# Top-2 gate dispatch on one Trainium2 core: loads with 32 KB rows, stores with 64 and 32 KB rows, and half of each group's output expanded in place over its own input

## Chip, core and metric

The kernel runs on one core of one Trainium2 chip. The metric is the device time of one execution in microseconds (us). A profile is one execution of the program taken by the hardware profiler; its span runs from the first to the last instruction on the core and is a little shorter than the device time of the same execution. KB and MB are used as the profile does: "2048.0 KB" of a DMA is 2,097,152 bytes, and 1 MB in a rate is a million bytes.

## Reference

The inputs are `x` (16 x 1024 tokens of 512 floats), router logits (8 per token) and k = 2. For each token the two largest softmax probabilities are taken and normalised to sum to 1, and the output holds the token's row twice, each copy multiplied by one of the two weights:

```python
    topk_indices = np.argsort(probs, axis=-1)[..., -k:]
    topk_probs = np.take_along_axis(probs, topk_indices, axis=-1)
    topk_probs = topk_probs / np.sum(topk_probs, axis=-1, keepdims=True)
    x_expanded = x[:, :, np.newaxis, :].repeat(k, axis=2)
    return (x_expanded * topk_probs[..., np.newaxis]).astype(np.float32)
```

So 33.55 MB of `x` and 0.52 MB of logits are read, and 67.11 MB are written, all in float32. Which expert was chosen does not enter the output; only the two weights do, and they are the sigmoids of the difference of the two largest logits.

## The kernel before

The 16,384 tokens are laid over 128 partitions with M = 128 tokens (slots) each, so that a partition's tokens are one contiguous stretch of memory: 256 KB of `x` and 512 KB of output.

**Weights (L22 to L42).** One DMA brings all logits into the core (L76). `top2_weights` finds the largest and second largest by a tree of max and min on VectorE (DVE), and two sigmoids on ScalarE (ACT) write the weight table `WA`. This is done once.

**Groups, loads and stores.** The work goes in two groups of 64 slots. In each group all eight loads are issued first: a load (L84) brings 8 slots, 128 rows of 16 KB, 2 MB, into its own buffer `xg` (a pool of eight). Then each buffer is expanded in two halves: one DVE multiplication (L90) reads 4 slots of `xg`, broadcast over k, times their weights, and writes 4 x 2 x 512 floats per partition into a buffer `og` (a pool of four, 16 KB a partition each); a store (L98) sends `og`, 128 rows of 16 KB, to the output. So a group is eight loads of 2 MB and then sixteen stores of 2 MB.

**What sets the order.** All DMAs, loads and stores alike, are issued by SyncE (SP) in program order, and run on one queue that is spread over the core's 16 DMA engines; each engine takes 8 of the 128 rows of each DMA. The order on SP is: logits, eight loads, sixteen stores, eight loads, sixteen stores. SP stops at the first instruction whose wait is not met, and everything behind it on SP stops with it. A store waits for its multiplication. A multiplication waits for its load, and for the store that last read its `og` buffer (four stores back). A load of the second group waits until the multiplications have read its buffer. No order is written out otherwise; the tile framework adds the waits. The pools take 8 x 16 + 4 x 16 = 192 KB a partition beside the weights.

Of the kernel before, what the change touches and what calls it, by code (L numbers as in the profile page):

```python
# [1 line left out]

# [4 lines left out]

F32 = mybir.dt.float32
ALU = mybir.AluOpType
ACTF = mybir.ActivationFunctionType  # L10
P = 128


def top2_weights(nc, pool, logits, M, E):

    hi, lo, n = None, None, E
    while n > 1:  # L20
        n //= 2
        if hi is None:  # L22
            a, b = logits[:, :, 0:n], logits[:, :, n : 2 * n]
            nhi = pool.tile([P, M, n], F32, tag=f"hi{n}")
            nlo = pool.tile([P, M, n], F32, tag=f"lo{n}")
            nc.vector.tensor_tensor(nhi, a, b, op=ALU.max)  # L26
            nc.vector.tensor_tensor(nlo, a, b, op=ALU.min)  # L27
        else:
            a, b = hi[:, :, 0:n], hi[:, :, n : 2 * n]
            nhi = pool.tile([P, M, n], F32, tag=f"hi{n}")  # L30
            nlo = pool.tile([P, M, n], F32, tag=f"lo{n}")
            tmp = pool.tile([P, M, n], F32, tag=f"tmp{n}")
            nc.vector.tensor_tensor(tmp, lo[:, :, 0:n], lo[:, :, n : 2 * n], op=ALU.max)  # L33
            nc.vector.tensor_tensor(nlo, a, b, op=ALU.min)  # L34
            nc.vector.tensor_tensor(nlo, nlo, tmp, op=ALU.max)  # L35
            nc.vector.tensor_tensor(nhi, a, b, op=ALU.max)  # L36
        hi, lo = nhi, nlo
    dlt = pool.tile([P, M], F32, tag="dlt")
    nc.vector.tensor_tensor(dlt, hi[:, :, 0], lo[:, :, 0], op=ALU.subtract)  # L39
    WA = pool.tile([P, M, 2], F32, tag="WA")  # L40
    nc.scalar.activation(WA[:, :, 0], dlt, ACTF.Sigmoid, scale=-1.0)  # L41
    nc.scalar.activation(WA[:, :, 1], dlt, ACTF.Sigmoid, scale=1.0)  # L42
    return WA


@with_exitstack
def kernel(
    ctx: ExitStack,
    tc: tile.TileContext,
    x: bass.AP,  # L50
    router_logits: bass.AP,
    k: bass.AP,
    out: bass.AP,
):
    nc = tc.nc
    B, S, D = x.shape
    E = router_logits.shape[-1]
    N = B * S
    assert int(k) == 2 and E == 8 and N % P == 0
    M = N // P  # L60

    L = 8
    H = 4
    GROUP = 8
    x_v = x.rearrange("b s d -> (b s) d").rearrange("(p m) d -> p m d", p=P)
    o_v = out.rearrange("b s k d -> (b s) k d").rearrange("(p m) k d -> p m k d", p=P)
    rl_v = router_logits.rearrange("b s e -> (b s) e").rearrange(
        "(p m) e -> p m e", p=P
    )

    wpool = ctx.enter_context(tc.tile_pool(name="wpool", bufs=1))
    xbufs = ctx.enter_context(tc.tile_pool(name="xbufs", bufs=GROUP))
    obufs = ctx.enter_context(tc.tile_pool(name="obufs", bufs=4))

    logits = wpool.tile([P, M, E], F32)
    nc.sync.dma_start(logits, rl_v)  # L76
    WA = top2_weights(nc, wpool, logits, M, E)

    for g in range(M // L // GROUP):
        chunks = range(g * GROUP, (g + 1) * GROUP)  # L80
        xgs = []
        for c in chunks:
            xg = xbufs.tile([P, L, D], F32, tag="xg")
            nc.sync.dma_start(xg, x_v[:, c * L : (c + 1) * L, :])  # L84
            xgs.append(xg)
        for c, xg in zip(chunks, xgs):
            for h in range(L // H):
                rows = slice(c * L + h * H, c * L + (h + 1) * H)
                og = obufs.tile([P, H, 2, D], F32, tag="og")
                nc.vector.tensor_tensor(  # L90
                    og,
                    xg[:, h * H : (h + 1) * H, :]
                    .unsqueeze(2)
                    .to_broadcast([P, H, 2, D]),
                    WA[:, rows, :].unsqueeze(3).to_broadcast([P, H, 2, D]),
                    op=ALU.mult,
                )
                nc.sync.dma_start(o_v[:, rows], og)  # L98


# [1 line left out]
_INS = ['x', 'router_logits', 'k']  # L102
_OUTS = [((16, 1024, 2, 512), 'float32')]

_NUMBERS = {'k': 2}


# [26 lines left out]
```

## Time and profile before

| | |
|---|---|
| median of 3 runs | 243.29 us (243.09 to 243.54) |
| the profiled execution's own time | 243.44 us |
| its span | 241.7 us |
| outside the span | 1.74 us |
| DMAs | 1 for the logits, 16 loads, 32 stores, all issued by SP |
| DVE busy | 144.8 us (60% of the span), of which L90 141.1 us in 32 instructions |
| bytes over the span | 101.2 MB, 419 GB/s on the mean |

How to read it. An engine's busy share is a mean over the whole span. The profile also cuts the span into 40 slices of 6.04 us and gives for each the busy share of the DMA engines and the GB/s that they moved; packets are counted by their start, so a slice can be a packet or two off. A DMA packet here is one row of one DMA on one engine: 6144 of the packets are the 16 KB rows of loads and stores, 128 are the 4 KB rows of the logits, and 16 small ones of 4 bytes end each DMA, one on each engine, and signal that the engine's share has landed. "To landing" is the time from a DMA's issue on SP until the last of these sixteen.

The trace also gives each DMA's landings by themselves. The loads of the first group land at 9.39, 14.29, 19.18, 24.08, 28.97, 33.86, 38.77 and 45.14 us, the stores behind them at 50.02, 54.88, 59.75, 64.60 us and so on up to 118.08 and 123.37; the second group's loads at 128.15, 133.05 and so on up to 157.52 and 163.01, and its stores from 167.88 to 240.81.

### The profile page before, as it was taken

To read this page: it belongs to the slowest core of one execution; us is meant where nothing else is said; L and a number is where in the kernel's file an instruction comes from. 1 tells how busy PE (TensorE), PEld (TensorE's weight loads), DVE (VectorE), ACT (ScalarE), POOL (GpSimd) and SP (SyncE) were. 2 spreads that over 40 slices of the span, in tenths; PEclk is the share of its full clock that TensorE was granted. 3 is DMA by queue.
4 is the path that set the end of the run, shared out by engine and by line. 5 is a ranking of instruction groups with operands and counts; after the bars stand their busy time and mean duration, and the time that the engine had idled before them with its cause. 6 is when DMAs were issued, how large, how long until landed. Compare 5 with 4: busy or idle time off the path is not lost.

```text
span 241.7 us, 202 instructions
## 1 busy us (share of the span) xinstructions
DVE 144.8 (60%) x43; ACT 1.8 (1%) x3; POOL 0.2 (0%) x4
## 2 busy tenths in 40 slices
DVE  2899400078999899980007991001998989989300
ACT  2000000000000000000000000000000000000000
POOL 0000000000000000000000000000000000000000
DMA  7999999999999999999999999999999999999995
GB/s 274 420 431 434 434 434 369 404 428 434 428 434 434 428 426 431 431 434 431 434 401 428 431 434 426 423 420 431 434 434 434 431 431 427 431 434 433 431 428 233
DMA packets 7058, 101.21 MB, mean 419 GB/s; under 512 B 784, under 2 KB 784, under 8 KB 912
## 3 DMA queue, kind: packets, MB, share of 16 engines
q1 hardware_dynamic: 7056, 101.19, 98.9%
q14 instruction: 2, 0.02, 0.0%
HBM read 34.08 MB, written 67.11 MB: 419 GB/s over the span
## 4 chain that ended last, share of the span: by engine, by line
DMA 74%; DVE 17%; issue 2%; SPq 1%; DVEq 0%
DMA out_dram<-og 61%; DVE og L90 17%; DMA xg<-in_x_dram 13%; SPq L84 0%; SPq L76 0%; SPq L98 0%; DVEq L90 0%
## 5 line engine op out<-in xcount | busy, mean ns | idle before, releaser
L90 DVE TENSOR_TENSOR og<-xg,WA 128x4096 f32<-128x4096 f32 x32 | 141.1, 4423 | 76.5 <-issue 45.5
L26 DVE TENSOR_TENSOR nhi<-logits 128x512 f32<-128x512 f32 x1 | 0.7, 691 | 4.6 <-DMA logits<-in_router_logits_dram 4.6
L41 ACT ACT_TABLE_LOAD x1 | 1.3, 1283 | 0.7 <-PEq L115 0.7
L36 DVE TENSOR_TENSOR nhi<-nhi 128x256 f32<-128x256 f32 (+1 forms) x2 | 0.7, 350 | 0.0
L34 DVE TENSOR_TENSOR nlo<-nhi 128x256 f32<-128x256 f32 (+1 forms) x2 | 0.7, 350 | 0.0
L33 DVE TENSOR_TENSOR tmp<-nlo 128x256 f32<-128x256 f32 (+1 forms) x2 | 0.7, 350 | 0.0
L35 DVE TENSOR_TENSOR nlo<-nlo,tmp 128x256 f32<-128x256 f32 (+1 forms) x2 | 0.7, 350 | 0.0
L27 DVE TENSOR_TENSOR nlo<-logits 128x512 f32<-128x512 f32 x1 | 0.7, 684 | 0.0
L41 ACT ACTIVATE WA<-dlt 128x128 f32<-128x128 f32 x1 | 0.3, 315 | 6.4 <-DVE dlt L39 6.4
L39 DVE TENSOR_TENSOR dlt<-nhi,nlo 128x128 f32<-128x128 f32 x1 | 0.3, 292 | 0.0
L42 ACT ACTIVATE WA<-dlt 128x128 f32<-128x128 f32 x1 | 0.3, 298 | 0.0
L115 POOL MEMSET const-uint8-127<- 128x1 uint8 x1 | 0.1, 103 | 0.0
L115 POOL MEMSET const-bfloat16-1.0<- 128x1 bf16 x1 | 0.1, 102 | 0.0
L115 POOL MEMSET const-float32-0.0<- 128x1 f32 x1 | 0.1, 99 | 0.2 <-issue 0.2
L115 POOL MEMSET const-float32-1.0<- 128x1 f32 x1 | 0.1, 99 | 0.0
## 6 DMA issues: line engine op xcount, KB each, us to landing
out_dram<-og SPq DMA_DIRECT2D x32, 2048.0 KB, 14.9
xg<-in_x_dram SPq DMA_DIRECT2D x16, 2048.0 KB, 28.8
logits<-in_router_logits_dram SPq DMA_DIRECT2D x1, 512.0 KB, 3.8
```

What stands on the lines that cost most here:

```text
L26: nc.vector.tensor_tensor(nhi, a, b, op=ALU.max)
L27: nc.vector.tensor_tensor(nlo, a, b, op=ALU.min)
L33: nc.vector.tensor_tensor(tmp, lo[:, :, 0:n], lo[:, :, n : 2 * n], op=ALU.max)
L34: nc.vector.tensor_tensor(nlo, a, b, op=ALU.min)
L35: nc.vector.tensor_tensor(nlo, nlo, tmp, op=ALU.max)
L36: nc.vector.tensor_tensor(nhi, a, b, op=ALU.max)
L39: nc.vector.tensor_tensor(dlt, hi[:, :, 0], lo[:, :, 0], op=ALU.subtract)
L41: nc.scalar.activation(WA[:, :, 0], dlt, ACTF.Sigmoid, scale=-1.0)
L42: nc.scalar.activation(WA[:, :, 1], dlt, ACTF.Sigmoid, scale=1.0)
L90: nc.vector.tensor_tensor(og, xg[:, h * H : (h + 1) * H, :] .unsqueeze(2) .to_broadcast([P, H, 2, D]), WA[:, rows, :].unsqueeze(3).to_broa ...
L115: nc = _bacc.Bacc("TRN2", target_bir_lowering=False, num_devices=1)
```

## The change

The buffers of the two pools become two tiles: `xs` of 64 slots (128 KB a partition) and `osp` of 16 slot pairs (64 KB a partition). A group is still 64 slots, with all loads ahead of all stores, on the same queue. Its loads are four DMAs of 16 slots, 128 rows of 32 KB, 4 MB each. Its expansion is six multiplications and six stores, by the list `plan`:

- slots 0 to 15 go to the whole of `osp`, one store with rows of 64 KB (8 MB);
- slots 16 to 31 go to `low`, which is `xs` slots 0 to 31 seen as 16 pairs: they are expanded over the slots 0 to 15 that the first step has read and over themselves; one store with rows of 64 KB;
- slots 32 to 39 go to the first half of `osp`, 40 to 47 to its second half; two stores with rows of 32 KB (4 MB);
- slots 48 to 55 go to `xs` slots 32 to 47, and 56 to 63 to `xs` slots 48 to 63, over what has been read and over themselves; two stores with rows of 32 KB.

`low` and `high` are views of `xs`, so a load of the second group waits for the store that reads its slots. The number of bytes, the elements multiplied and the weights are the same.

```diff
-    L = 8
-    H = 4
-    GROUP = 8
+    GROUP = 64
+    L = 16
...
-    xbufs = ctx.enter_context(tc.tile_pool(name="xbufs", bufs=GROUP))
-    obufs = ctx.enter_context(tc.tile_pool(name="obufs", bufs=4))
-
...
-    for g in range(M // L // GROUP):
-        chunks = range(g * GROUP, (g + 1) * GROUP)
-        xgs = []
-        for c in chunks:
-            xg = xbufs.tile([P, L, D], F32, tag="xg")
-            nc.sync.dma_start(xg, x_v[:, c * L : (c + 1) * L, :])
-            xgs.append(xg)
-        for c, xg in zip(chunks, xgs):
-            for h in range(L // H):
-                rows = slice(c * L + h * H, c * L + (h + 1) * H)
-                og = obufs.tile([P, H, 2, D], F32, tag="og")
-                nc.vector.tensor_tensor(
-                    og,
-                    xg[:, h * H : (h + 1) * H, :]
-                    .unsqueeze(2)
-                    .to_broadcast([P, H, 2, D]),
-                    WA[:, rows, :].unsqueeze(3).to_broadcast([P, H, 2, D]),
-                    op=ALU.mult,
-                )
-                nc.sync.dma_start(o_v[:, rows], og)
+    xs = wpool.tile([P, GROUP, D], F32)
+    osp = wpool.tile([P, L, 2, D], F32)
+
+
+    low = xs[:, : 2 * L, :].rearrange("p (r k) d -> p r k d", k=2)
+    high = xs[:, 2 * L :, :].rearrange("p (r k) d -> p r k d", k=2)
+    h = L // 2
+    plan = [
+        (0, L, osp),
+        (L, L, low),
+        (2 * L, h, osp[:, :h]),
+        (2 * L + h, h, osp[:, h:]),
+        (3 * L, h, high[:, :h]),
+        (3 * L + h, h, high[:, h:]),
+    ]
+
+    for g in range(M // GROUP):
+        m0 = g * GROUP
+        for r in range(0, GROUP, L):
+            nc.sync.dma_start(xs[:, r : r + L, :], x_v[:, m0 + r : m0 + r + L, :])
+        for r, n, og in plan:
+            rows = slice(m0 + r, m0 + r + n)
+            nc.vector.tensor_tensor(
+                og,
+                xs[:, r : r + n, :].unsqueeze(2).to_broadcast([P, n, 2, D]),
+                WA[:, rows, :].unsqueeze(3).to_broadcast([P, n, 2, D]),
+                op=ALU.mult,
+            )
+            nc.sync.dma_start(o_v[:, rows], og)
```

## The prediction

> **What bounds the kernel now.** I read the page's slices first, then rates by stage, then the multiplications in order of time. The slices:
>
> ```profile
> DVE  2899400078999899980007991001998989989300
> ...
> DMA  7999999999999999999999999999999999999995
> GB/s 274 420 431 434 434 434 369 404 428 434 428 434 434 428 426 431 431 434 431 434 401 428 431 434 426 423 420 431 434 434 434 431 431 427 431 434 433 431 428 233
> ```
>
> The DMA engines are never idle from the second slice to the last but one, and move about 431 GB/s; DVE has holes. The low slices are the start (0), the end (39), and the places where the queue goes from loads to stores (6 and 7) and from stores to loads (20). The same by stage (columns: stretch, length, busy us of DVE, ACT, POOL, TensorE clock, DMA share, GB/s):
>
> ```profile
> 12.00:38.00 26.00, 14.92 (x4) 0.00 (x0) 0.00 (x0) 1.00 1.01 433
> 38.00:46.00 8.00, 0.00 (x0) 0.00 (x0) 0.00 (x0) 1.00 0.99 358
> 46.00:118.00 72.00, 53.10 (x12) 0.00 (x0) 0.00 (x0) 1.00 1.01 431
> 118.00:128.00 10.00, 0.00 (x0) 0.00 (x0) 0.00 (x0) 1.00 1.01 413
> 128.00:156.00 28.00, 17.43 (x4) 0.00 (x0) 0.00 (x0) 1.00 1.01 431
> 156.00:168.00 12.00, 0.04 (x1) 0.00 (x0) 0.00 (x0) 1.00 1.00 422
> 168.00:236.00 68.00, 53.06 (x12) 0.00 (x0) 0.00 (x0) 1.00 1.01 431
> ```
>
> Against 431, the changes of direction lose 8 x (1 - 358/431) = 1.35 us, 10 x (1 - 413/431) = 0.42 and 12 x (1 - 422/431) = 0.25: about 2.0 in all. In between, the order of time shows DVE waiting for stores, not stores for DVE:
>
> ```profile
> 54.97 4.42 DVE L90 TENSOR_TENSOR og<-xg,WA 128x4096 f32<-128x4096 f32 x1 [0.44 <-DMA out_dram<-og]
> 59.83 4.42 DVE L90 TENSOR_TENSOR og<-xg,WA 128x4096 f32<-128x4096 f32 x1 [0.43 <-DMA out_dram<-og]
> 64.69 4.43 DVE L90 TENSOR_TENSOR og<-xg,WA 128x4096 f32<-128x4096 f32 x1 [0.44 <-DMA out_dram<-og]
> ```
>
> The starts are 4.86 us apart, the time of one 2 MB store. So the bytes through the DMA engines are the bound: 101.2 MB at 431 GB/s is 234.8 us of the 241.7. The change moves the same bytes. Only the cost per packet and per DMA, the direction changes, and a gap in the queue, if it makes one, can matter.
>
> **Cost per packet.** In the trace's packet records, on one engine, the commonest distance from one 16 KB store packet to the next is 607 ns, and for the 4 KB rows of the logits 155 ns. The slope is (607 - 155)/12,288 bytes: 602.7 ns for 16 KB, which leaves 4.3 ns fixed per packet. Loads: their landings are 4.895 us apart, 611.9 ns per packet, 9.2 over the slope, and I do not know whether that excess goes with packets or with bytes. Between the last packet of one DMA and the first of the next the distance is mostly 613, so a DMA's end costs some 6 ns.
>
> Each engine has 8 rows of each DMA. Loads: 16 x 8 = 128 packets before, 8 x 8 = 64 after, 64 fewer: 64 x 4.3 = 0.28 us, or 64 x 9.2 = 0.59 if the loads' whole excess is per packet. Stores: 32 x 8 = 256 before; after, 4 with 64 KB rows and 8 with 32 KB rows, 12 x 8 = 96, 160 fewer: 160 x 4.3 = 0.69. DMAs: 49 before, 21 after, 28 x 6 ns = 0.17. Sum 1.14 to 1.45; I take 1.3. No row of this trace shows a packet above 16 KB. From below: if rows are cut at 16 KB, only the 0.17 is left. From above on this term: 1.45.
>
> The Trainium skill, "DMA: Bandwidth & Descriptors", section "Anatomy of one DMA", gives a transfer a fixed 2.0 us beside its bytes; 28 fewer would be worth 56 us, an estimate from that page, and the time 187. That section itself says that it is completion latency; in this trace stores follow each other 4.86 us apart for 8 x 602.7 ns = 4.82 us of bytes, so 0.04 us of it is on the path here. The page's section "Why small descriptors are slow" has about 3 cycles of overhead per packet, which with its 850 MHz is an estimate of 3.5 ns, and 224 fewer packets would give 0.79 us in place of the 0.97 (0.28 + 0.69) from the rows.
>
> **DVE.** Per output element (4423 - 691)/(4096 - 512) = 1.041 ns from the rows of L90 and L26, fixed 0.16 us. A step of 16 slots (16,384 outputs) is 17.2 us, of 8 slots 8.7: 4 x 17.2 + 8 x 8.7 = 138.4 in place of 141.1. All of it lies beside DMAs, so it counts nothing as long as the queue stays fed. Writing over one's own input: L35 does it (nlo<-nlo,tmp), 350 ns, as L33 and L34, which do not:
>
> ```profile
> L33 DVE TENSOR_TENSOR tmp<-nlo 128x256 f32<-128x256 f32 (+1 forms) x2 | 0.7, 350 | 0.0
> L35 DVE TENSOR_TENSOR nlo<-nlo,tmp 128x256 f32<-128x256 f32 (+1 forms) x2 | 0.7, 350 | 0.0
> ```
>
> I take no extra; L35 is small and not broadcast, so bound it by twice the step (8.7 more for 8 slots), which the margins below still cover.
>
> **Does the queue stay fed?** Larger steps mean later first stores and longer waits, so I lay the six steps (S0 to S5) out at the old rates: 64 KB stores 19.4 us, 32 KB stores 9.7, loads 9.8. Load 0 lands at 14.3 (where before the second load did). S0's multiplication ends at 31.5, S1's at 48.7. Loads end at 45.1 with the old loss of the direction change. S0's store, issued at 31.5, has 13 us in hand; it lands at 64.5, and S1's, issued at 48.7, follows to 84.0. S2 writes `osp` and must wait until S0's store has landed: this is the wait that the change adds. Behind it on DVE stand S3, S4, S5, and on SP their stores and all loads of the second group. It runs 64.6 to 73.3, and the queue needs it at 84.0: **margin 10.7 us**, the smallest of all. S3 ends at 82.0, S4 at 90.7, S5 at 99.4; their stores are needed at 93.7, 103.4, 113.1. SP then issues the second group's loads 0 and 1 at about 99.5 (their slots were freed when S1's store landed, 84.0); load 2 waits for S4's store (113.1), load 3 for S5's (122.9), with load 0 and 1 (19.6 us) queued ahead. The second group repeats it: load 0 lands near 133, S0 is multiplied by 150.3, loads end at 163; S2 runs 182.5 to 191.2 and is needed at 201.9. SP's own issues, 12 stores of 0.33 us and 8 loads of 0.47 us, are fewer than before. No margin is under 8.7, so even a doubled 8-slot step in S2 would not empty the queue. If this cover went, each microsecond past 10.7 would be lost twice, once a group.
>
> **What stays.** The start (load 0's data begins as before, behind the logits) and the tail: sixteen parts of the last store land from 238.86 to 240.81, a spread of 1.95 us that the slowest engine sets. These are the same in kind; I allow 0.5 either way.
>
> **Sum.** The profiled execution's own 243.44 (span 241.7 and 1.74 around it) less 1.3 is 242.1. The median of the runs lies 0.15 below the profiled one; from it, 243.29 - 1.3 = **242.0**, which I take.
>
> **Rivals.**
> - *The rows do not become larger packets*, or the excess goes with bytes. For: every 16 KB row is one packet, but nothing larger is seen. Against: the 4 KB and 16 KB rows differ as a fixed cost would make them. Then only 0.17 goes: 243.1.
> - *Slower: the direction changes grow with the row.* After the first group's loads each engine's first three or so store packets take 0.85 to 1.25 us in place of 0.61. If that is a loss per packet, with 64 KB rows it is four times as long where stores follow loads, 3 x (1.35 + 0.25) = 4.8 more, and with 32 KB rows twice where loads follow stores, 0.42 more: 242.0 + 5.2 = 247.2; at half of that 244.6. It decides for slower from 1.3 + 0.5 = 1.8 us extra, when the 2.0 of before becomes 3.8. Against it: the second change from loads to stores costs only 0.25 with the same rows, so it looks like engines that start in step and get out of each other's way in time, not like a price per packet.
> - *Faster than forecast: the first direction change shrinks* to the second's price, as longer rows change how engines meet: 1.1 less, 240.9. Nothing shows it but the 1.35 against 0.25.
>
> **How the numbers follow.** A difference of 0.2% (0.49 us) is about what a measurement of this kernel can tell from no change; so faster means below 242.8, slower above 243.8. Forecast (241.3 to 242.8): 0.58. No larger packets (242.8 to 243.8): 0.15. Direction changes grow: 0.17. They shrink: 0.10. Faster 0.58 + 0.10 = 0.68, same 0.15, slower 0.17. The range takes in the forecast, the no-gain case, the shrinking case down to 240.7 and the start of the slower case: 240.7 to 244.0, leaving out most of the slower case and little else.
>
> **What would show it.** Right: packet count near 2,560 beside the small ones; rates of 432 to 434 GB/s between the direction changes; no hole in the DMA row; DVE idle before S2, ended by a store. Wrong: 6,144 large packets (first rival); rates under 400 for more than 4 us around 45 and 160 us (second); a slice with DMA under 9 in the middle, which would mean that a margin above was misjudged.

## The result and the profile after

Beside the prediction's 242.0 us (240.7 to 244.0) the changed kernel took 242.67 us in the median of 4 runs (242.31 to 242.96), the kernel before 243.19 (242.86 to 243.54) next to it: ratio 0.9978, interval 0.9958 to 0.9997. With more runs even that shrank. In the next comparison (11 runs against 28) the two took 242.57 and 242.48 us, ratio 1.0001, interval 0.999 to 1.0012. The two intervals overlap only between 0.999 and 0.9997. So a gain of 0 to 0.1% is all that fits both, under what a measurement of this kernel can tell from no change; the forecast was 0.5%.

The profiled execution of the changed kernel was the fastest of its four (242.31 us, span 240.5), so the first thing to learn is not to read the gain from one pair of profiles (1.1 us here). The slices, with the page's packet count:

```profile
DVE  3279999900399999400000899998007999990000
...
DMA  8999999898989899999999999999989898999995
GB/s 327 430 409 425 430 431 425 349 523 349 523 349 523 349 436 436 436 436 431 436 338 431 436 431 430 431 474 414 458 381 490 371 501 360 431 436 436 436 436 256
DMA packets 3024, 101.19 MB, mean 421 GB/s; under 512 B 336, under 2 KB 336, under 8 KB 464
```

3024 - 464 = 2560 large packets: the rows did become packets of 32 and 64 KB. The DMA row has no hole. The pairs of 349 and 523 are not a rate: packets are counted by their start, and with 64 KB packets a slice holds two or three rounds of them. Slice 20 (338) is the change from stores to loads, and it is lower than before. By stage (stretch, length, busy us of DVE, ACT, POOL, clock, DMA share, GB/s):

```profile
12.00:38.00 26.00, 24.17 (x2) 0.00 (x0) 0.00 (x0) 1.00 1.01 435
38.00:46.00 8.00, 8.00 (x1) 0.00 (x0) 0.00 (x0) 1.00 1.02 360
46.00:118.00 72.00, 36.96 (x5) 0.00 (x0) 0.00 (x0) 1.00 1.00 433
118.00:128.00 10.00, 0.00 (x0) 0.00 (x0) 0.00 (x0) 1.00 0.99 370
128.00:156.00 28.00, 22.94 (x2) 0.00 (x0) 0.00 (x0) 1.00 1.00 432
156.00:168.00 12.00, 11.51 (x1) 0.00 (x0) 0.00 (x0) 1.00 1.02 437
168.00:236.00 68.00, 34.67 (x4) 0.00 (x0) 0.00 (x0) 1.00 1.00 432
```

Between the changes of direction the rate is 432 to 435, where the kernel before has 431 to 433 (forecast 432 to 434). The stretch with the change from stores to loads fell from 413 to 370. And the multiplications in order of time, with the group lines:

```profile
63.95 17.29 DVE L97 TENSOR_TENSOR osp<-xs,WA 128x8192 f32<-128x8192 f32 x2 [15.67 <-DMA out_dram<-osp]
...
181.60 17.29 DVE L97 TENSOR_TENSOR osp<-xs,WA 128x8192 f32<-128x8192 f32 x2 [14.10 <-DMA out_dram<-osp]
```

```profile
L97 DVE TENSOR_TENSOR osp<-xs,WA 128x8192 f32<-128x8192 f32 (+1 forms) x6 | 69.0, 11534 | 70.1 <-DMA xs<-in_x_dram 40.3
L97 DVE TENSOR_TENSOR xs<-xs,WA 128x8192 f32<-128x8192 f32 (+1 forms) x6 | 69.2, 11536 | 0.2
```

S2 waits 14 to 16 us for S0's store, starts at 63.95 (forecast 64.6) and is done at 72.6, with its store's turn at about 83. Writing in place costs nothing: 11,536 ns in xs, 11,534 in osp.

**The measure used below.** Rates in a window blur with long packets, so I use the landings in the trace. The *loss* at a change of direction is counted over two DMAs, the last of the old direction and the first of the new: how much longer they take together, by their landings, than in steady running (4.89, 9.72 and 19.35 us for loads of 2, 4 and 8 MB, 4.86, 9.68 and 19.32 for stores; where the last DMA is cut into short pieces, over all its pieces). In the changed kernel, for example, the third load lands at 33.14 us, the fourth at 44.54 and the first store at 63.85; that is 30.7 us in place of 29.0, a loss of 1.7, nearly all of it before the last load lands. Loads of 4 MB land 9.68 to 9.73 us apart, so a loss is good to some 0.03 us. There are three changes: loads to stores, stores to loads, loads to stores.

### The profile page after: what moved, and what is told of

The parts are those of the page before. It is cut to its first block, busy times and chain, and to the rows that moved or that the text cites. A ratio compares the mean times of both kernels' runs of the same rounds, so it can differ in the third digit from the quotient of the medians.

```text
span 240.5 us, 112 instructions
## 1 busy us (share of the span) xinstructions
DVE 142.0 (59%) x23; ACT 1.8 (1%) x3; POOL 0.2 (0%) x4
## 2 busy tenths in 40 slices
DMA packets 3024, 101.19 MB, mean 421 GB/s; under 512 B 336, under 2 KB 336, under 8 KB 464
## 3 DMA queue, kind: packets, MB, share of 16 engines
q1 hardware_dynamic: 3024, 101.19, 98.7%
## 4 chain that ended last, share of the span: by engine, by line
DMA 46%; DVE 36%; issue 7%; SPq 0%; DVEq 0%
DMA out_dram<-osp 27%; DVE osp L97 22%; DMA xs<-in_x_dram 19%; DVE xs L97 14%; SPq L72 0%; SPq L103 0%; DVEq L97 0%
## 5 line engine op out<-in xcount | busy, mean ns | idle before, releaser
L97 DVE TENSOR_TENSOR osp<-xs,WA 128x8192 f32<-128x8192 f32 (+1 forms) x6 | 69.0, 11534 | 70.1 <-DMA xs<-in_x_dram 40.3
L97 DVE TENSOR_TENSOR xs<-xs,WA 128x8192 f32<-128x8192 f32 (+1 forms) x6 | 69.2, 11536 | 0.2
```

What stands on the lines that cost most here:

```text
L97: nc.vector.tensor_tensor(og, xs[:, r : r + n, :].unsqueeze(2).to_broadcast([P, n, 2, D]), WA[:, rows, :].unsqueeze(3).to_broadcast([P, n, ...
```

## Why there was no gain

Taking the losses, and the time until the logits land, out of the last landing leaves the pace. Profiles of the kernel before, and of a version of the changed kernel with all rows at 16 KB (rows16 below), against those of the changed kernel (us):

| | logits land | losses in order | sum of losses | last landing | last landing less logits and losses |
|---|---|---|---|---|---|
| before | 4.56 | 1.50, 0.31, 0.58 | 2.39 | 240.81 | 233.86 |
| before_again | 4.38 | 0.69, 0.73, 0.07 | 1.49 | 239.82 | 233.95 |
| rows16 | 4.58 | 0.42, 0.54, 0.13 | 1.09 | 239.57 | 233.90 |
| after | 4.02 | 1.70, 1.34, 0.15 | 3.19 | 239.53 | 232.32 |
| after_again | 4.46 | 0.88, 1.21, 0.58 | 2.67 | 239.48 | 232.35 |

The last column is the part that the forecast worked out: 1.6 us less, 1.14 to 1.45 forecast, and it is there in each execution. The losses take it back: 1.66 on the mean of the three, 2.93 with the long rows, 1.27 more. The 0.3 us between the two are inside the scatter of the losses. Of the 1.27, the change from stores to loads has 0.75; the other 0.5 lies in the changes from loads to stores, where two executions of one kernel differ by as much (1.50 and 0.69), so these profiles do not show that the long rows caused that part. In the first pair of profiles another 0.5 us came from the logits landing early (4.02), which none of the eighteen later profiles repeats (4.22 to 4.64).

The experiments ask what sets these losses. Theory A: the rows next to the change. Theory B: chance. Theories C, D and E came up on the way. Ratios are to the kernel before on the same chip, with the 95% interval.

## Experiments: the change from stores to loads

**Both kernels again.** No edit.

> The unchanged kernel before, to see how far one execution of it differs from the next. Both theories: ratio 1.000 within 0.002. Theory A (the rows set the price of the change from stores to loads): the last store of the first group lands 5.2 to 5.4 us after the one before it, as in the first profile (5.29), a loss of 0.3 to 0.5. Theory B (the direction changes and the start scatter from one execution to the next, whatever the rows): this loss lies anywhere between 0.3 and 1.5, and the first load's landing (9.39 in the first profile) moves by up to 0.8.

> The changed kernel once more. Theory A: 0.4 to 0.7 us under the kernel before in the median; the last store of the first group lands about 11.1 us after the one before it in place of 9.69 (loss 1.2 to 1.6 again); loads and stores in between keep 9.72, 9.68 and 19.32 us; the first load lands between 13.4 and 14.3. Theory B: the same median, but the loss at that place somewhere between 0.3 and 1.5, and not tied to it.

Measured: before_again 242.41 us, 0.9995 (0.9986 to 1.0005); after_again 242.57, 1.0001 (0.999 to 1.0012). The loss from stores to loads is 0.31 and 0.73 in the two executions before, 1.34 and 1.21 in the two after. The first load's landing moved by only 0.1 in the kernel before. That speaks for A at this place; the losses from loads to stores scatter as B says (1.50 and 0.69; 1.70 and 0.88).

**The last store of each group in 16 KB rows (laststore, laststore_again).**

```diff
-            nc.sync.dma_start(o_v[:, rows], og)
+            if r == 3 * L + h:
+                for s in range(0, n, 4):
+                    nc.sync.dma_start(o_v[:, m0 + r + s : m0 + r + s + 4], og[:, s : s + 4])
+            else:
+                nc.sync.dma_start(o_v[:, rows], og)
```

> The changed kernel with the last store of each group cut into two stores with 16 KB rows. Theory A in the form that it is the stores' rows: the loss at the change from stores to loads falls from 1.5 to 0.4 to 0.8, so the time is 0.6 to 1.0 us under the changed kernel (16 more packets an engine and 2 more DMAs cost 0.08 of it). Theory A in the form that it is the loads' rows, and theory B: the time is that of the changed kernel plus 0.1, within 0.2.

> The kernel with 16 KB rows in the last store of each group, once more, beside the three below. Theory A (the price of a change of direction grows with the rows next to it): ratio to the kernel before 0.996 to 0.998 as the first time (0.9970); loss from stores to loads 0.5 to 0.9. If the first time was chance: 0.999 to 1.001.

**The first load of each group in 16 KB rows (firstload).**

```diff
-            nc.sync.dma_start(xs[:, r : r + L, :], x_v[:, m0 + r : m0 + r + L, :])
+            step = 8 if r == 0 else L
+            for s in range(r, r + L, step):
+                nc.sync.dma_start(
+                    xs[:, s : s + step, :], x_v[:, m0 + s : m0 + s + step, :]
+                )
```

> The changed kernel with the first load of each group cut into two loads with 16 KB rows. Theory A in the form that it is the loads' rows: the loss at the change from stores to loads falls from 1.5 to 0.4 to 0.8 and the time is 0.6 to 1.0 us under the changed kernel (16 more packets an engine and 2 more DMAs cost 0.1 to 0.15 of it). Theory A in the form of the stores' rows, and theory B: the time of the changed kernel plus 0.1 to 0.2.

Measured: laststore 241.77 us, 0.997 (0.9959 to 0.9982), and 241.70, 0.9977 (0.9966 to 0.9987); loss 0.70 and 0.70. firstload 242.57, 1.0007 (0.9998 to 1.0016); loss 1.26. So it is the stores' rows and not the loads'; with 4 MB of each group's 32 cut, the kernel is 0.4 to 0.7 us under the kernel before.

**Longer and shorter last stores (all64, laststore4, turns).** all64 replaces the last four steps by two with 64 KB rows; laststore4 cuts the last store into 4, 2, 1 and 1 slots; turns does that too and cuts the last load into 8, 4, 2, 1 and 1 slots, which is rows of 16, 8, 4, 2 and 2 KB (its expectation below names them twice, the second time rightly).

```diff
+        (2 * L, L, osp),
+        (3 * L, L, high),
...
+            cuts = (4, 2, 1, 1) if r == 3 * L + h else (n,)
...
+            cuts = (8, 4, 2, 1, 1) if r == 3 * L else (L,)
```

> The changed kernel with four stores a group, all with 64 KB rows: slots 32 to 47 over the whole of osp, 48 to 63 over the last half of xs. Theory A (the last stores' rows price the change from stores to loads): the loss there grows from 1.5 to 2.2 to 3.0 us; 32 fewer packets an engine and 4 fewer DMAs give 0.15 back; so 0.5 to 1.4 us over the changed kernel, about 243.0 to 244.0 where the kernel before has 242.5. Theory B (scatter): the changed kernel less 0.15. The third store's multiplication has 2.3 us in hand by the old times; if that is misjudged, the DMA row shows a hole near 84 us and it is that.

> The changed kernel with the last store of each group cut into rows of 16, 8, 4 and 4 KB (4, 2, 1 and 1 slots). Theory A: the loss at the change from stores to loads falls to 0.2 to 0.6 (0.86 with 16 KB rows, 1.5 with 32 KB); 0.1 to 0.6 under the kernel with 16 KB last stores, so a ratio to the kernel before of 0.9945 to 0.9968. Theory B or a fixed price per change: ratio 0.997 as with 16 KB last stores, or 0.0005 more for the packets and DMAs added.

> As with the last stores of 16, 8, 4 and 4 KB rows, and the last load of each group cut too, into 32, 16, 8, 4 and 4 ... slots of 8, 4, 2, 1 and 1 (rows of 16, 8, 4, 2 and 2 KB). Theory A for both directions: the losses from loads to stores (0.8 to 1.7 and 0.1 to 0.8 with 32 KB loads) fall by half or more, 0.4 to 1.0 us under the kernel with the cut last stores alone, ratio to the kernel before 0.991 to 0.994. If the price from loads to stores lies with the first 64 KB stores, it stays, and the time is that of the cut last stores plus 0.05 to 0.1.

Measured: all64 244.30 us, 1.0075 (1.0062 to 1.0087), somewhat over what A expected, loss 2.40, and no hole at 84 us; its two losses from loads to stores are also large in this execution (1.2 and 1.1). laststore4 242.18, 0.9987 (0.9978 to 0.9997), loss 0.87; turns 242.09, 0.9981 (0.9972 to 0.9991), loss 0.90. So in these runs the loss with 16, 32 and 64 KB is 0.3 to 0.7, 1.2 to 1.3 and 2.4 us, and theory B is out for this change. Below 16 KB it does not fall further, which A had wrong. The losses from loads to stores in turns are about 0.4 to 0.6 and 0.2 to 0.3 (laststore4: 1.3 and 0.7), as A expected, but the forecast time, 0.991 to 0.994, was missed: the cut loads are 64 packets an engine more, and at the 9.2 ns that a load's packet costs beside its bytes these are 0.6 us, an estimate. The rate over 30 us around the change, in before_again, after_again, laststore_again and all64 in this order (last number):

```profile
108.00:138.00 30.00, 10.26 (x3) 0.00 (x0) 0.00 (x0) 1.00 1.01 423
```

```profile
108.00:138.00 30.00, 5.46 (x1) 0.00 (x0) 0.00 (x0) 1.00 1.01 417
```

```profile
108.00:138.00 30.00, 5.78 (x1) 0.00 (x0) 0.00 (x0) 1.00 0.99 423
```

```profile
108.00:138.00 30.00, 3.96 (x1) 0.00 (x0) 0.00 (x0) 1.00 0.98 404
```

In the packet records of after_again, on most engines the last 32 KB store packet takes 1.65 to 2.05 us in place of 1.21, and the three load packets behind it 1.2 to 1.8.

**All rows back to 16 KB (rows16).** Each load in two, each store in two or four DMAs; tiles, steps and writing in place stay.

```diff
+            for s in range(r, r + L, 8):
+                nc.sync.dma_start(xs[:, s : s + 8, :], x_v[:, m0 + s : m0 + s + 8, :])
...
+            for s in range(0, n, 4):
+                nc.sync.dma_start(o_v[:, m0 + r + s : m0 + r + s + 4], og[:, s : s + 4])
```

> The changed kernel with every DMA cut back to 16 KB rows (16 loads, 32 stores); the six multiplications a group, the two tiles and the writing in place stay. Theory A (only the rows matter): the time of the kernel before, ratio 0.999 to 1.001; loads 4.89 us and stores 4.86 apart, losses at the changes of direction as before (0.4 to 0.9 from stores to loads). Rival C (the order of the multiplications or the writing in place costs something): more than 0.3 us over the kernel before.

Measured: 242.51 us, 1.0007 (0.9998 to 1.0016). The pace in the table (233.90) is that of the kernel before, and by the interval the six steps and the writing in place cost at most 0.4 us by themselves; nothing speaks for theory C.

## Experiments: the change from loads to stores

**Shorter and longer last loads (lastload, bothlast, load64).** lastload cuts the last load in two with 16 KB rows, bothlast the last load and the last store, load64 makes two loads a group with 64 KB rows.

```diff
+            step = 8 if r == 3 * L else L
+            for s in range(r, r + L, step):
...
+        for r in range(0, GROUP, 2 * L):
+            nc.sync.dma_start(xs[:, r : r + 2 * L, :], x_v[:, m0 + r : m0 + r + 2 * L, :])
```

> The changed kernel with the last load of each group cut into two loads with 16 KB rows; the stores stay as changed. Theory A for this direction too: the two losses from loads to stores, 0.8 to 1.7 and 0.1 to 0.8 with 32 KB rows, fall together by 0.4 to 0.8, the loss from stores to loads stays at 1.2 to 1.4; ratio to the kernel before 0.997 to 0.999. If only the last stores' rows matter: the time of the changed kernel plus 0.1, ratio 1.000 to 1.001.

> Both cuts, the last load and the last store of each group with 16 KB rows, all else as changed. Theory A: all three losses as before the change, the saving per packet kept: 0.9 to 1.3 us under the kernel before, ratio 0.9945 to 0.9963. If only the last stores' rows matter: 0.997 as with that cut alone.

> The changed kernel with two loads a group, rows of 64 KB. Theory A for this direction: each loss from loads to stores grows, together from 1.7 (1.2 and 0.5) to 2.4 to 4.0 us, against 32 fewer packets an engine that give 0.2 to 0.3; 0.5 to 2.0 us over the changed kernel, ratio to the kernel before 1.002 to 1.008. If the loads' rows do not matter: 0.2 to 0.3 us under the changed kernel, ratio 0.999 to 1.000. The first store is issued at about 41 us, 2 us before the loads end; a hole in the DMA row there would add to the loss and be seen.

Measured: lastload 242.38 us, 1.0007 (0.9998 to 1.0016), losses from loads to stores 1.52 and 0.53: no help. bothlast 241.49, 0.9967 (0.9955 to 0.998), no better than the cut last store alone by its interval. load64 **240.62, 0.993** (0.9918 to 0.9943), where A had it slower: both losses from loads to stores are 0.04. So A, by which longer rows lose more, falls for this direction. load64 differs in two things: the rows, and the moment of the first store. Its first multiplication must wait for an 8 MB load, so the first store goes on the queue at 41 us, 2 us before the loads end, and not at 31. Theory D: the moment. Theory E: the rows.

**The moment alone, the rows alone (swap01, early64).** swap01 issues the first two loads in the other order; early64 keeps the first two loads and joins the last two into one with 64 KB rows.

```diff
-        for r in range(0, GROUP, L):
+        for r in (L, 0, 2 * L, 3 * L):
...
+        for r, c in ((0, L), (L, L), (2 * L, 2 * L)):
+            nc.sync.dma_start(xs[:, r : r + c, :], x_v[:, m0 + r : m0 + r + c, :])
```

> The changed kernel with the first two loads of each group issued in the other order (slots 16 to 31, then 0 to 15). The bytes, rows and stores are the same, but the first multiplication starts one load later, so the first store is issued at about 40.6 us, 2 us before the loads end, in place of 31. Theory D (a change of direction costs when the new direction stands on the queue early): the two losses from loads to stores (1.2 and 0.5 on the mean) go to 0 to 0.2, so 1.2 to 1.8 us under the changed kernel, ratio to the kernel before 0.992 to 0.995. Theory E (the loads' rows must not be shorter than the stores'): the time of the changed kernel, ratio 1.000 to 1.001.

> The changed kernel with the last two loads of each group made into one with 64 KB rows; the first two stay, so the first store is issued at 31 us as in the changed kernel. Theory E (row length): the losses from loads to stores go to 0 to 0.2, ratio 0.992 to 0.995. Theory D (the moment): they stay or grow, 1.5 to 3.0 together, ratio 0.999 to 1.005.

Measured: swap01 **240.96 us, 0.9944** (0.9932 to 0.9955), losses 0.03 and 0.06. early64 242.39, 1.0009 (0.9999 to 1.0019), losses 1.78 and 1.14. The first store's issue in the order of time (start, length), and then the same DMA among the issues (last number: us to landing). In after_again:

```profile
31.54 0.35 SPq L103 DMA_DIRECT2D out_dram<-osp  x1
```

```profile
out_dram<-osp SPq DMA_DIRECT2D x1, 32.0
```

In swap01:

```profile
41.23 0.35 SPq L103 DMA_DIRECT2D out_dram<-osp  x1
```

```profile
out_dram<-osp SPq DMA_DIRECT2D x1, 21.4
```

In early64:

```profile
31.34 0.35 SPq L103 DMA_DIRECT2D out_dram<-osp  x1
```

```profile
out_dram<-osp SPq DMA_DIRECT2D x1, 32.8
```

The first store lands at 63.5, 62.6 and 64.1 us: the one issued ten microseconds later lands first. D holds, E falls.

**The same order with an early store again; late stores with short rows (swap_half, rows16_swap).** swap_half cuts the first step of swap01 into two of 8 slots; rows16_swap is rows16 with the loads in swap01's order.

```diff
-        (0, L, osp),
+        (0, h, osp[:, :h]),
+        (h, h, osp[:, h:]),
```

> The kernel with the first two loads in the other order, but its first multiplication and store of each group cut into two of 8 slots (32 KB rows), so that a first store is issued at about 32.6 us, 10 us before the loads end, and the second at 41.3. Theory D (the moment): the losses from loads to stores come back, 0.8 to 2.0 together, ratio to the kernel before 0.998 to 1.002. If the other order of the loads itself removed them: they stay near 0, ratio 0.994 to 0.996.

> All rows cut back to 16 KB, with the first two 16-slot pieces of each group loaded in the other order, so that the first store is issued at about 41.3 us. Theory D: the losses from loads to stores go to 0 to 0.2 with these rows too, so about 1.1 us under the kernel before, ratio 0.9945 to 0.9965. Against the kernel with the same order and the changed rows (0.9944) the 1.3 us per packet are missing and some 0.7 us from stores to loads are saved, so it should lie 0.3 to 0.7 us over it, 0.9957 to 0.9973. If the moment matters for long rows only: 1.000.

Measured: swap_half 242.41 us, 1.000 (0.9991 to 1.0009), losses 1.13 and 0.25. Its first store is on the queue at 32.59 and the gain is gone, so it is the moment and not the order of the loads:

```profile
32.59 0.35 SPq L104 DMA_DIRECT2D out_dram<-osp  x1
```

No run cut the first stores alone with the loads in the changed kernel's order, so whether their 64 KB rows make an early store dearer is not shown. Next, rows16_swap: 243.59, 1.0049 (1.0036 to 1.0063): its losses from loads to stores are indeed gone (-0.01 and 0.01), but it is slower than the kernel before, a miss of 2 us. Two things appear in its trace: the loss from stores to loads is 1.41 (0.54 in rows16), and the first group's stores are 4.90 us apart where rows16 has 4.86. The same stretch in rows16 and rows16_swap, last number:

```profile
46.00:118.00 72.00, 37.76 (x5) 0.00 (x0) 0.00 (x0) 1.00 1.01 431
```

```profile
46.00:118.00 72.00, 47.27 (x5) 0.00 (x0) 0.00 (x0) 1.00 1.01 427
```

With the saved losses taken off, these two put its last landing 0.7 us later than in rows16 in the profile; the medians differ by 1.1. By the mean of the sixteen parts of each store the pace is 4.90 us in both groups (4.86 in both of rows16). In the second group the last parts hide it, because the sixteen parts draw together, from 0.9 us apart to 0.2. Why short rows lose pace there, and lose 1.41 at a change that cost 0.3 to 0.8 in the other runs with such rows, is open.

**A late first load, and both cures (lateload, load64_ls16).** lateload cuts the last store into 6 and 2 slots and lets the second group begin with the slots that the 6-slot store reads, so that this load is issued at 119.21 us, 2.7 us before the stores end. load64_ls16 is load64 with laststore's edit.

```diff
+        if g:
+            order = ((3 * L, 12), (0, L), (L, L), (2 * L, L), (3 * L + 12, 4))
...
+            cuts = (6, 2) if r == 3 * L + h else (n,)
```

> The changed kernel with the last store of each group cut into 6 and 2 slots (rows of 24 and 8 KB) and the second group's loads issued as slots 48 to 59, 0 to 15, 16 to 31, 32 to 47, 60 to 63, so that the first of them waits for the 6-slot store to land and is issued some 2 us before the stores end, in place of 23. Theory D for this direction: the loss from stores to loads falls from 1.25 to 0 to 0.4; 0.8 to 1.2 us under the changed kernel, ratio 0.995 to 0.997, and more if the second change from loads to stores profits from a first store issued at 157 us (5 us before the loads end). Theory E: the loss follows the last stores' rows, 0.4 to 0.8 with 8 KB rows, ratio 0.997 to 0.998. If the loads come too late, the DMA row has a hole near 122 us and the time is that of the changed kernel or more.

> The kernel with 64 KB loads, and the last store of each group cut into two with 16 KB rows. The last stores' rows price the change from stores to loads: 0.4 to 0.8 in place of 1.5, so 0.6 to 1.0 us under the kernel with 64 KB loads alone, ratio to the kernel before 0.9885 to 0.991. If 64 KB loads behind them price it: as the kernel with 64 KB loads, 0.993.

Measured: lateload 242.55 us, 1.002 (1.0009 to 1.0031): loss from stores to loads 0.88, and no hole in the DMA row. The moment does not remove the loss in this direction. At its second change from loads to stores the first store is on the queue at 156.87 us, 5 us before the loads end, and the loss is still 0.59 (its last load has rows of 8 KB); so 5 us was not late enough in this run, and 2 us was in four. load64_ls16 **240.39, 0.9923** (0.991 to 0.9935), losses 0.04, 0.77 and 0.04. It beats both kernels, by 0.8%. The time missed its forecast (0.9885 to 0.991), and against load64 alone the intervals overlap, but the loss from stores to loads fell from 1.53 to 0.77 as forecast.

**Stores to loads over all the runs.** With 32 KB last stores the loss is 1.0 to 1.5 us in eight profiles, with 16 KB 0.3 to 0.8 in seven and 1.41 in rows16_swap. So the last stores' rows matter, but they do not set the loss alone. Within each set it tends to be smaller where the first change from loads to stores lost more: 1.0 in early64 and lastload, where that lost 1.8 and 1.5, and 1.5 in swap01 and load64, where it lost nothing. It looks as if a loss that is saved at one change comes back in part at the next; but this is a tendency over sixteen profiles (1.7 and 1.3 in the first profile of the changed kernel lie off it), and no run tested it.

## Why the prediction was wrong, step by step

- **What bounds the kernel: right.** The DMA engines' bytes, in every profile.
- **Cost per packet: right.** The prediction's 4.3 ns and its slope give 1209.7 and 2415 ns for 32 and 64 KB; the commonest distances in the trace are 1209 and 2414. 2,560 packets as forecast. The term came out at 1.6 us against 1.14 to 1.45 (1.3 taken); the loads' excess did go with packets. The 2.0 us per DMA that the prediction quotes from the Trainium skill, "DMA: Bandwidth & Descriptors", section "Anatomy of one DMA", is fitted there to DMAs that GpSimd issues, and these are issued by SyncE.
- **DVE and the queue's cover: right, but for one margin.** Steps of 17.23 and 8.70 us, no hole, no extra for writing in place. The prediction held that its margins cover in-place steps of twice the length. They did not: the in-place steps are S1, S4 and S5, not S2, and doubled they end S1 at 65.9 us, after its store's turn at 64.5, and S5 at 118.1, after 113.1. Writing in place cost nothing, so it made no difference, but that bound was wrong.
- **"What stays" and the sum: here the forecast failed.** "What stays" names only the start and the tail, and the sum takes the changes of direction over at their old 2.0 us (2.4 by landings) without a reason; their growth stood only as a rival with 0.17. The rival happened, at a quarter of its price: 1.27 us more, not 5.2, too little for its "slower" (1.8 extra) and enough to eat the gain. The part from stores to loads grew from 0.5 to 1.3, in step with the last stores' rows up to 64 KB (2.4). The rival put most of its price on the other direction, and there growth is not shown. Its sign of being wrong, rates under 400 around 45 us, could not tell either: the kernel before has 358 there already, and the changed one 360; the fall came around 123 us, 413 to 370.
- **Two readings behind that were wrong.** The slow packets after the first group's loads were called store packets. In the changed kernel sizes tell them apart: in after_again they are the last one or two 32 KB load packets of each engine (up to 2.05 us in place of 1.21), and the 64 KB store packets behind them run at 2.42 from the first on. And the 0.25 at the second change from loads to stores was taken as a property of that change; the runs scatter there from 0.07 to 0.58 with the same rows.
- **One profile as a scale.** The three losses of the kernel before, 2.39 in the profile that I read, were 1.49 in the next execution, and 1.09 in rows16 with the same rows. A term of 1.3 us was set against a term whose own scatter is as large.

The Trainium skill, "DMA: Bandwidth & Descriptors", section "Two DMAs through the same engine are not ordered", says that within one queue descriptors start in order but are pipelined, and that an engine's read and write sides are separate queues. That would let a store that already stands on the queue begin its reads while the last loads still write, and the runs fit it: a first loss of 0.4 to 1.8 us with the store queued 10 us or more before the loads end (at the second change 0.07 to 1.1), 0.59 in the one with 5, none over 0.06 with 2. No run shows the two sides themselves, and the page does not say why the other direction follows the row length, so the mechanism stays open. Shown are two causes: the moment, from loads to stores; and the last stores' rows, from stores to loads in the changed kernel and in load64 (laststore twice, load64_ls16, all64). rows16_swap shows that the second is not the only one in its direction.

## What to carry to other kernels

Where the DMA queue is the bound and always full, look at the places where it changes between loads and stores: there the order of issue and the rows next to the change are worth as much as the cost of all packets together. Try not to put the first store on the queue long before the loads end if it can be had late without a gap (0.6% here, for one changed loop), and to keep the last stores before a load short (16 KB rows in place of 32 gave 0.2 to 0.3% twice, and beside 64 KB loads 0.1%, inside the intervals). Measure it each time: with 16 KB rows throughout, the late store made the kernel 0.4% slower. A saving that repeats in every packet is easy to forecast; set it against the scatter of the losses over several profiles before calling it a gain.

## What the runs showed that was not expected

- A DMA issued later landed earlier: first store issued at 41.23 us, landed at 62.6 (swap01); issued at 31.54, landed at 63.5 (after_again).
- Once no change from loads to stores cost anything, row length mattered far more: with the same late order 1.0049 with 16 KB rows and 0.9944 with the changed ones, some 1% between them, although with early stores the same two row lengths differ by less than 0.1%.
- Rows under 16 KB in the last stores (down to 4 KB) did not lower the loss from stores to loads any further: 0.87 and 0.90 against 0.70.
